# Two product chunks of a feed-forward stage: down products one step later, first factors split early, token halves exchanged, freed banks to the end of the line, two low parts on VectorE

## The chip, the cores and the metric

The kernel runs on one core of one Trainium2 chip. TensorE multiplies, VectorE (DVE in the profile) and ScalarE (ACT) split and combine, GpSimd (POOL) and SyncE (SP) start transfers. The metric is the device time of one execution, in microseconds (us).

## The reference

The program is a trunk of two layers. Each layer is feed-forward, mixer (mLSTM in layer 0, gated MLP in layer 1), feed-forward, gated embedding, each followed by a layer norm. So there are four feed-forward stages, and the change lies in these alone:

```python
def swiglu_ffn(x, w_gu, w_d):
    g, u = jnp.split(x @ w_gu, 2, axis=-1)
    return (jax.nn.silu(g) * u) @ w_d

x = layer_norm(DN_ALPHA * x + 0.5 * swiglu_ffn(x, ffn1_wgu[i], ffn1_wd[i]), ln_g[i, 0], ln_b[i, 0])
```

x has 512 tokens and 1024 columns, the hidden width is 2816. All is float32.

## The kernel before, in words

**Splitting.** A float32 matrix is used as a high and a low part. ScalarE copies the source rounded (whi of a weight, fhi of a factor; L237, L323), VectorE subtracts that from the source (wlo, flo; L246, L324). A product takes three matmuls, high by high, low by high and high by low (`mm3`, L318 to L320). A low can be made without VectorE: ScalarE copies the negated high (L243), and a transfer started by GpSimd adds the source to it (L244). `UP_BY_DMA` lists the weight forms made in that way.

**Weights.** `Weights.order` is one list of all weight tiles in the order in which TensorE takes them. Whenever a tile is released, `fill` splits the next ones in this order until a kind has no free buffer. There are four buffers of the kind main (up weights) and two of the kind rows (down weights). Loads go through three raw buffers (wraw) and five quarters (wquarter), and a raw buffer is loaded anew when the last form made from it is split.

**A feed-forward stage.** The 22 hidden blocks of 128 go through in chunks of 2, 4, 4, 4, 4, 4. While a chunk is projected up, the seven products of the chunk before it go down; these are a Strassen scheme (`Group`: `form` makes and splits a factor, `product` multiplies, `add` puts the result on the residual xt, L687). Down products are called D0 to D6 here. Chunks 0 to 3 are projected plainly. Chunks 4 and 5, here the product chunks, project a pair of blocks in seven products, r0 to r6, and a chunk has two pairs (`UpPair`, `up_products`). So a product chunk has 14 steps s = 0 to 13 of one up product each, and seven of them have a down product too: before, those with even s. The activations' side of the up products is made once at the end of chunk 3 (`UpForms`; its `last` is a row of VectorE work with the tiles x_d, t_wlo and t_f).

**Banks.** r0, r2, r4 and r6 of a pair add into one bank, r3 and r5 into another, r1 has one. After r0, r2 and r3 ScalarE copies the bank out (tile us, L972), after r1, r5 and r4 VectorE adds it to such a copy (L975, L980), ScalarE applies Silu (L976), and VectorE makes h for a half of the tokens by `gated` (L989): after r5 for one half, after r6 for the other. The next product in a bank waits for the copy out of it: r2 for that after r0, r4 for that after r2, r5 for that after r3. In chunk 5 the two halves are split into high and low at once (wquarter, L323, L324). Then `down` multiplies its four blocks plainly, 128 tokens at a time, into dps, after which norm and the next stage follow. The first 128 tokens' dps use the two down banks that `add` of D5 gave free, the second those that `add` of D6 gives free.

**What sets the order.** Nothing is scheduled: each engine runs its instructions in the order in which the Python code emits them, one after the other, and waits at the head of its queue. In `up_products` a step emits the up product, the pending `add`, the copy out or Silu (`take`), the fills of the released up weight, and with a down product that product, the fills of the released down weight, and the next `form`. Both first forms of the next group were emitted at a chunk's end, for chunk 3 behind `UpForms.last`.

Weight forms are made in place on VectorE: s2 (L139, L140) for r2, s3 (L147) for r4, s4 (L151) for r5; for the down weights t2 (L110, L111) for D2 and t1 (L115, L116) for D3.

Of the kernel before, what the change touches and what calls it, by code (L numbers as in the profile page):

```python
# [42 lines left out]
W_BUFS = 4  # L43
EXTRA = 2
PLE_EXTRA = 3
UP_BY_DMA = (1, 2, 4, 5, 6)


class Weights:
# [238 lines left out]
def hybrid_trunk(ctx: ExitStack, tc, x, p, ln_g, ln_b, ffn1_wgu, ffn1_wd, ffn2_wgu, ffn2_wd,  # L288
# [39 lines left out]
    up_held = set()  # L328

    def up_bank(name, hold=False):  # L330
# [7 lines left out]
            return i, bank  # L338
        return bank

    dn_order, pinned = deque(range(4)), {}

    def dn_bank(name, pin=False):
# [57 lines left out]
    def ffn_weights(wgu, wd, name, ple=False):  # L401
# [19 lines left out]
        for c, n in enumerate(FFN_CHUNKS):  # L421
            down_w = deque(forms(c - 1) if c else ())
            if c >= UP_FROM:
                products = []
                for b in range(starts[c], starts[c] + n, 2):
                    products += W.up_forms(*(W.add_load(kp(wgu)[:, :, c0:c0 + 2 * P], 2) for c0 in (b * P, HID + b * P)))
                for s, product in enumerate(products):
                    W.order.append(product)
                    if s % 2 == 0:
                        W.order.append(down_w.popleft())  # L430
                continue
            for i in range(2 * n):
                W.order.append(tiles[2 * starts[c] + i])
                if down_w:
                    W.order.append(down_w.popleft())
# [450 lines left out]
    class UpForms:  # L886
# [52 lines left out]
                          self.quarter(1, 1), self.t4]  # L939

        def quarter(self, k, t):
            return [a[:, 4 * k:4 * k + 4, 256 * t:256 * t + 256] for a in (xh, xl)]

        def step(self):
            if self.steps:
# [2 lines left out]
    class UpPair:  # L948
# [19 lines left out]
        def take(self, r):  # L968
            bank, part = self.bank, self.part
            if r in (0, 2, 3):  # L970
                part[r] = tmp_tile("us").rearrange("p (e c) -> p e c", e=2)
                sca.activation(part[r], bank[3 if r == 3 else 0], AF.Copy)  # L972
            elif r in (1, 5):
                g = part[r // 5 * 2]
                vec.tensor_add(g, g, bank[1 if r == 1 else 3])  # L975
                sca.activation(g, g, AF.Silu)  # L976
                if r == 5:
                    self.gated(1, g, part[3])
            elif r == 4:
                vec.tensor_add(part[3], part[3], bank[0])  # L980
            else:
                self.gated(0, part[0], bank[0])
            if r in (1, 5, 6):
                up_held.remove(self.at[{1: 1, 5: 3, 6: 0}[r]])

        def gated(self, t, g, u):
            s = slice(256 * t, 256 * t + 256)
            h = g if self.h is None else self.h[:, :, s]
            vec.scalar_tensor_tensor(h, g, 0.5, u, op0=OP.mult, op1=OP.mult)  # L989
            if self.h is None:  # L990
# [3 lines left out]
    def ffn(layer, k, rows, late, prepare=None):  # L994
        with stage_pool("forms", 2) as fpool, stage_pool("quarters", Q_BUFS) as qpool, \
# [16 lines left out]

            def up_products(c, n, h):
                nonlocal norm
                pairs = []
                for s in range(7 * n // 2):
                    b, r = s // 7 * 2, s % 7
                    if r == 0:
# [5 lines left out]
                        hs.extend([a[:, e] for a in pair.parts] for e in range(2))  # L1024
                    pair.take(r)
                    W.release()
                    if s % 2 == 0:
                        group.product()
                        W.release(kind="rows")
                        group.form()  # L1030
                    if c == LAST and b == n - 2:
                        if r == 2:
                            W.open("rowsx", late, 1)
                        elif r == 4:
                            norm = Norm(layer, k)

            for c, n in enumerate(FFN_CHUNKS):
                if c < LAST:
# [3 lines left out]
                if c == UP_FROM - 1:  # L1042
                    formed = UpForms(tpool, late)
                if c >= UP_FROM:
                    up_products(c, n, h if c < LAST else None)
                for i in range(2 * n if c < UP_FROM else 0):
                    b = i // 2
                    ps = project()
# [20 lines left out]
                    if formed is not None and i >= FORM_AT:  # L1069
                        formed.step()  # L1070
                        formed.step()
                if c == UP_FROM - 1:
                    while formed.steps:
                        formed.step()
                    formed.last()
                if c < LAST:
                    group = Group(h, fpool, c == 0)
                    group.form()
                    group.form()
# [730 lines left out]
```

## Time and profile before

| | |
|---|---|
| median of 3 runs | 2334.89 us (2334.58 to 2336.22) |
| the profiled execution | 2333.96 us |
| its span, first to last instruction | 2332.2 us |
| TensorE busy, VectorE, ScalarE | 96%, 72%, 46% |
| mean granted TensorE clock | 0.980 |
| product chunks of the four stages begin at | 212.89, 998.79, 1433.56, 2091.42 us |

The trace gives for every instruction its start, its duration and the idle time of its engine before it with what ended that (in brackets). A row with x2 or more merges instructions of one kind that follow each other. TensorE's rows overlap, since its matmuls are pipelined: the distance from start to start is what one costs.

### The profile page before, as it was taken

To read this page: it belongs to the slowest core of one execution; us is meant where nothing else is said; L and a number is where in the kernel's file an instruction comes from. 1 tells how busy PE (TensorE), PEld (TensorE's weight loads), DVE (VectorE), ACT (ScalarE), POOL (GpSimd) and SP (SyncE) were. 2 spreads that over 40 slices of the span, in tenths; PEclk is the share of its full clock that TensorE was granted. 3 is DMA by queue.
4 is the path that set the end of the run, shared out by engine and by line. 5 is a ranking of instruction groups with operands and counts; after the bars stand their busy time and mean duration, and the time that the engine had idled before them with its cause. 6 is when DMAs were issued, how large, how long until landed. Compare 5 with 4: busy or idle time off the path is not lost. (4 is left out here: it accounts for less than half of the span.)

```text
span 2332.2 us, 29478 instructions
## 1 busy us (share of the span) xinstructions
PE 2231.4 (96%) x11669; PEld 1909.1 (82%) x11669; DVE 1678.9 (72%) x2436; ACT 1081.3 (46%) x1508; POOL 172.5 (7%) x215
## 2 busy tenths in 40 slices
PE   9998998999999999989899998898999999999888
PEld 8887887888888888878788887887888888878777
DVE  5668676786776776777786768676788767687777
ACT  4334555564646533355454334554345453346542
POOL 1000110111101000001000000110001000001000
PEclk9999999999999999999999999999999999999999
DMA  6324753556847443356532323753437733346551
GB/s 202 109 82 117 179 112 127 135 128 137 163 113 147 133 130 100 104 122 157 151 122 93 122 70 108 181 131 123 136 90 149 176 101 109 100 118 139 142 161 56
DMA packets 217842, 295.70 MB, mean 127 GB/s; under 512 B 7092, under 2 KB 161844, under 8 KB 217704
## 3 DMA queue, kind: packets, MB, share of 16 engines
q1 hardware_dynamic: 168080, 211.83, 27.9%
q0 software_dynamic: 43008, 67.30, 17.8%
q10 hardware_dynamic: 6616, 14.69, 2.1%
q8 instruction: 92, 1.51, 0.3%
q14 instruction: 46, 0.38, 0.1%
HBM read 224.58 MB, written 2.11 MB: 97 GB/s over the span
## 5 line engine op out<-in xcount | busy, mean ns | idle before, releaser
L237 ACT ACTIVATE whi<-wraw 128x1024 fp32r<-128x1024 f32 (+1 forms) x388 | 400.1, 1047 | 193.4 <-DVE wraw L140 50.4
L246 DVE TENSOR_TENSOR wlo<-wraw,whi 128x1024 fp32r<-128x1024 f32 (+1 forms) x260 | 312.2, 1216 | 81.3 <-ACT whi L237 80.5
L246 DVE TENSOR_TENSOR wlo<-wquarter,whi 128x1024 fp32r<-128x1024 f32 (+1 forms) x140 | 156.4, 1117 | 246.7 <-ACT whi L237 246.5
L318 PE MATMUL fps<-xh,whi 128*128 128x512 f32 x800 | 311.4, 389 | 0.0
L319 PE MATMUL fps<-xl,whi 128*128 128x512 f32 x800 | 311.2, 389 | 0.0
L320 PE MATMUL fps<-xh,wlo 128*128 128x512 f32 x800 | 311.2, 389 | 0.0
L318 PE MATMUL gps<-whi,fhi 128*128 128x512 f32 x644 | 260.0, 404 | 34.9 <-ACT fhi L323 34.9
L320 PE MATMUL gps<-whi,flo 128*128 128x512 f32 x644 | 258.8, 402 | 11.6 <-DVE flo L324 11.6
L319 PE MATMUL gps<-wlo,fhi 128*128 128x512 f32 x644 | 258.3, 401 | 0.0
L244 POOL DMA_DIRECT2D wlo<-wraw x128 | 127.8, 998 | 1560.5 <-ACT wlo L243 1406.2
L237 ACT ACTIVATE whi<-wquarter 128x1024 fp32r<-128x1024 f32 (+1 forms) x140 | 135.7, 969 | 225.2 <-PE gps L320 109.3
L687 DVE TENSOR_TENSOR xt<-xt,gps 128x512 f32<-128x512 f32 x302 | 192.9, 679 | 0.8 <-PE gps L320 0.8
L318 PEld LDWEIGHTS fps<-xh,whi 128*128 128x128 f32 x800 | 150.2, 188 | 31.2
L319 PEld LDWEIGHTS fps<-xl,whi 128*128 128x128 f32 x800 | 150.2, 188 | 31.1
L320 PEld LDWEIGHTS fps<-xh,wlo 128*128 128x128 f32 x800 | 150.1, 188 | 31.1
L318 PEld LDWEIGHTS gps<-whi,fhi 128*128 128x128 f32 x644 | 125.1, 194 | 61.0 <-ACT fhi L323 36.6
L323 ACT ACTIVATE fhi<-h 128x512 fp32r<-128x512 f32 (+1 forms) x140 | 81.1, 582 | 202.3 <-DVE h L852 53.0
L320 PEld LDWEIGHTS gps<-whi,flo 128*128 128x128 f32 x644 | 124.7, 194 | 44.3 <-DVE flo L324 17.3
L318 PE MATMUL ups<-xh,whi 128*128 128x256 f32 x512 | 146.6, 286 | 6.4 <-DVE us L989 4.3
L320 PE MATMUL ups<-xh,wlo 128*128 128x256 f32 x512 | 146.5, 286 | 2.3 <-DMA wlo<-wraw 2.1
L319 PEld LDWEIGHTS gps<-wlo,fhi 128*128 128x128 f32 x644 | 125.3, 195 | 24.9
L319 PE MATMUL ups<-xl,whi 128*128 128x256 f32 x512 | 145.5, 284 | 0.0
(357 smaller groups left out, 4945.4 us busy)
## 6 DMA issues: line engine op xcount, KB each, us to landing
wraw<-in_ffn_wgu_dram SPq DMA_DIRECT2D x79, 1024.0 KB, 7.3
wlo<-wraw POOLq DMA_DIRECT2D x128, 512.0 KB, 5.5
wquarter<-in_ffn_wd_dram SPq DMA_DIRECT2D x64, 512.0 KB, 3.8
wraw<-in_ml_w_in_dram SPq DMA_DIRECT2D x24, 1024.0 KB, 5.9
wraw<-in_gm_w_in_dram SPq DMA_DIRECT2D x15, 1024.0 KB, 5.6
wraw<-in_ffn_wgu_dram SPq DMA_DIRECT2D x17, 512.0 KB, 4.8
wraw<-in_ffn_wd_dram SPq DMA_DIRECT2D x8, 1024.0 KB, 9.1
wraw<-in_ml_w_out_dram SPq DMA_DIRECT2D x8, 1024.0 KB, 5.0
```

Source lines behind the costliest of these rows:

```text
L237: self.nc.scalar.activation(hi[:, s], src[:, s], AF.Copy)
L244: self.nc.gpsimd.dma_start(lo[:, s], src[:, s], accum_op=OP.add)
L246: self.nc.vector.tensor_sub(lo[:, s], src[:, s], hi[:, s].bitcast(F32))
L318: mm(ps, st[0], mv[0], start=start, stop=False, skip_group_check=more)
L319: mm(ps, st[0], mv[1], start=False, stop=False, skip_group_check=more)
L320: mm(ps, st[1], mv[0], start=False, stop=stop, skip_group_check=more)
L323: sca.activation(hi, src, AF.Copy)
L687: vec.tensor_add(dst, dst, ps)
```

## The change

- `UP_BY_DMA` loses forms 5 and 6: the lows of r5 and r6 are subtracted on VectorE. There are two product chunks with two pairs in each of four stages, so 32 lows move.
- In the product chunks the down products (and their weights in `Weights.order`) stand at odd s, one step later. D6 is now the last product of the chunk, and its `add` comes behind the chunk.
- The first factor of the next group is formed early: in chunks 1 to 3 at i = 6, in chunk 4 at s = 12. The second is formed at the chunk's end, for chunk 3 ahead of `UpForms.last`.
- `quarter` and `gated` exchange the token halves: what r5 completes is now tokens 0 to 255.
- `up_let_go` puts a freed up bank at the end of the line, where before its place was that of its last taking.

```diff
-UP_BY_DMA = (1, 2, 4, 5, 6)
+UP_BY_DMA = (1, 2, 4)
...
+    def up_let_go(i):
+        up_held.remove(i)
+        up_order.remove(i)
+        up_order.append(i)
...
                 for s, product in enumerate(products):
                     W.order.append(product)
-                    if s % 2 == 0:
+                    if s % 2:
                         W.order.append(down_w.popleft())
...
         def quarter(self, k, t):
-            return [a[:, 4 * k:4 * k + 4, 256 * t:256 * t + 256] for a in (xh, xl)]
+            return [a[:, 4 * k:4 * k + 4, 256 - 256 * t:512 - 256 * t] for a in (xh, xl)]
...
             if r in (1, 5, 6):
-                up_held.remove(self.at[{1: 1, 5: 3, 6: 0}[r]])
+                up_let_go(self.at[{1: 1, 5: 3, 6: 0}[r]])
...
         def gated(self, t, g, u):
-            s = slice(256 * t, 256 * t + 256)
+            s = slice(256 - 256 * t, 512 - 256 * t)
...
                     pair.take(r)
                     W.release()
-                    if s % 2 == 0:
+                    if s % 2:
                         group.product()
                         W.release(kind="rows")
                         group.form()
+                    if s == 12 and h is not None:
+                        next_group = Group(h, fpool)
+                        next_group.form()
...
                 if c >= UP_FROM:
-                    up_products(c, n, h if c < LAST else None)
+                    next_group = up_products(c, n, h if c < LAST else None)
+                    if c < LAST:
+                        next_group.form()
+                    group.add()
+                    group = next_group
...
+                    if c and i == 6:
+                        next_group = Group(h, fpool)
+                        next_group.form()
+                if c < UP_FROM and c:
+                    group = next_group
+                    group.form()
                 if c == UP_FROM - 1:
                     while formed.steps:
                         formed.step()
                     formed.last()
-                if c < LAST:
+                if c == 0:
                     group = Group(h, fpool, c == 0)
                     group.form()
                     group.form()
```

How this moves the instructions is shown at three places. Line numbers of the changed kernel are larger by 5 from `up_let_go` to `up_products` (L687 is L692, L989 is L994), and by other amounts behind that.

The first is VectorE at the start of chunk 4 of the first stage, behind `UpForms.last`. Before:

```order
L932 TENSOR_TENSOR t_wlo<-x_f_1300,t_whi 128x1024
L324 TENSOR_TENSOR t_f_1754<-x_d,t_f_1753 128x512 x2
L324 TENSOR_TENSOR flo<-h,fhi 128x512 x2
L147 TENSOR_TENSOR wraw<-wraw 128x1024
L110 TENSOR_TENSOR wquarter<-wquarter 128x1024
L111 TENSOR_TENSOR wquarter<-wquarter 128x1024
L246 TENSOR_TENSOR wlo<-wquarter,whi 128x1024
L851 TENSOR_TENSOR h<-h 128x2x256
L852 TENSOR_TENSOR h<-h 128x2x256
L324 TENSOR_TENSOR flo<-h,fhi 128x512
```

The same place in the changed kernel:

```order
L937 TENSOR_TENSOR t_wlo<-x_f_1300,t_whi 128x1024
L324 TENSOR_TENSOR t_f_1762<-x_d,t_f_1761 128x512 x2
L147 TENSOR_TENSOR wraw<-wraw 128x1024
L980 TENSOR_TENSOR us<-us,ups 128x512
L151 TENSOR_TENSOR wraw<-wraw 128x1024
L246 TENSOR_TENSOR wlo<-wraw,whi 128x1024
L110 TENSOR_TENSOR wquarter<-wquarter 128x1024
L111 TENSOR_TENSOR wquarter<-wquarter 128x1024
L246 TENSOR_TENSOR wlo<-wquarter,whi 128x1024
L856 TENSOR_TENSOR h<-h 128x2x256
L857 TENSOR_TENSOR h<-h 128x2x256
L324 TENSOR_TENSOR flo<-h,fhi 128x512
```

Both first flo of the group have gone ahead of this place; the addition after r1 (L980), the form of r5's weight (L151) and its low, which VectorE did not make before, now stand ahead of D2's weight and factor.

The second is ScalarE at the same place, from the first copy out of a bank (us, after r0) to the second (after r2). Before:

```order
L972 ACTIVATE us<-ups 128x512
L237 ACTIVATE whi<-wraw 128x1024
L243 ACTIVATE wlo<-wraw 128x1024
L237 ACTIVATE whi<-wquarter 128x1024
L323 ACTIVATE fhi<-h 128x512
L976 ACTIVATE us<-us 128x512
L237 ACTIVATE whi<-wraw 128x1024
L243 ACTIVATE wlo<-wraw 128x1024
L972 ACTIVATE us<-ups 128x512
```

In the changed kernel:

```order
L977 ACTIVATE us<-ups 128x512
L237 ACTIVATE whi<-wraw 128x1024
L243 ACTIVATE wlo<-wraw 128x1024
L981 ACTIVATE us<-us 128x512
L237 ACTIVATE whi<-wraw 128x1024
L237 ACTIVATE whi<-wquarter 128x1024
L323 ACTIVATE fhi<-h 128x512
L977 ACTIVATE us<-ups 128x512
```

Silu (L981) and the high of r5's weight have moved ahead of D2's weight and factor, one low is gone, and the copy after r2 now follows directly on the factor fhi.

The third is VectorE at the end of chunk 5, up to the first dps on the residual. Before:

```order
L989 SCALAR_TENSOR_TENSOR us<-us 128x512
L324 TENSOR_TENSOR wquarter<-us,wquarter 128x2x256
L246 TENSOR_TENSOR wlo<-wraw,whi 128x1024 x4
L687 TENSOR_TENSOR xt<-xt,gps 128x512 x2
L989 SCALAR_TENSOR_TENSOR us<-us,ups 128x512
L324 TENSOR_TENSOR wquarter<-us,wquarter 128x2x256
L246 TENSOR_TENSOR wlo<-wraw,whi 128x1024
L687 TENSOR_TENSOR xt<-xt,dps 128x512
```

In the changed kernel:

```order
L994 SCALAR_TENSOR_TENSOR us<-us 128x512
L324 TENSOR_TENSOR wquarter<-us,wquarter 128x2x256
L994 SCALAR_TENSOR_TENSOR us<-us,ups 128x512
L324 TENSOR_TENSOR wquarter<-us,wquarter 128x2x256
L246 TENSOR_TENSOR wlo<-wraw,whi 128x1024 x5
L692 TENSOR_TENSOR xt<-xt,gps 128x512 x2
L692 TENSOR_TENSOR xt<-xt,dps 128x512
```

The second half of h is made and split ahead of the weight lows, and the residual of D6 (xt from gps) now comes behind five of them.

More of the change, by code (lines that the diff above doesn't have):

```diff
@@ L1014, in up_products @@
                 nonlocal norm
-                pairs = []
                 for s in range(7 * n // 2):
@@ L1035, in up_products @@
                             norm = Norm(layer, k)
+                return next_group if h is not None else None
             for c, n in enumerate(FFN_CHUNKS):
```

## The prediction

> **What bounds the kernel now.** I read the page's busy times first, then what TensorE waits for, then the queues of TensorE, VectorE and ScalarE through the product chunks.
>
> ```profile
> span 2332.2 us, 29478 instructions
> PE 2231.4 (96%) x11669; PEld 1909.1 (82%) x11669; DVE 1678.9 (72%) x2436; ACT 1081.3 (46%) x1508; POOL 172.5 (7%) x215
> ...
> PE gps L318 <- ACT fhi L323: 34.9, 8, 5.5
> PE dps L318 <- ACT wquarter L323: 21.5, 4, 5.8
> PE gps L320 <- DVE flo L324: 11.6, 8, 2.4
> PE ups L318 <- ACT us L972: 9.1, 14, 1.3
> PE ups L320 <- DMA wlo<-wraw: 8.6, 8, 2.1
> PE ups L318 <- DVE us L989: 4.3, 4, 1.3
> ```
>
> TensorE waits 90.0 us in these six rows (total, times, longest), all inside the product chunks and just behind them. The change aims at each row: a step more before D0 at the factors (34.9 + 11.6), the exchanged halves at the down pass (21.5), VectorE's lows at the transfers (8.6), the bank line at the last row (4.3). Long waits cost more than they show:
>
> ```profile
> 221.45 0.80 PE L318 MATMUL gps<-whi,fhi 128*128 128x512 f32 x1 [5.53 <-ACT fhi L323]
> ...
> 224.43 0.63 PE L319 MATMUL gps<-wlo,fhi 128*128 128x512 f32 x1
> 224.85 0.63 PE L320 MATMUL gps<-whi,flo 128*128 128x512 f32 x1
> ...
> 331.31 0.40 PE L319 MATMUL gps<-wlo,fhi 128*128 128x512 f32 x1
> 331.55 0.39 PE L320 MATMUL gps<-whi,flo 128*128 128x512 f32 x1
> ...
> 335.24 0.39 PE L318 MATMUL ups<-t_whi,whi 128*128 128x256 f32 x1 [1.25 <-ACT us L972]
> 335.46 0.28 PE L319 MATMUL ups<-t_wlo,whi 128*128 128x256 f32 x1
> 335.58 0.28 PE L320 MATMUL ups<-t_whi,wlo 128*128 128x256 f32 x1
> ```
>
> After 5.53 us of waiting a 512-column matmul takes 0.42 from start to start, against 0.24 in a steady stretch; after 1.25 the 256-column ones soon go at 0.12. From these distances 12 matmuls of a down product take 5.0 slow and 2.8 at full speed, so a long wait costs TensorE some 2 to 3 more: with 12 long waits, some 30. If nothing took their place, 120 would go. The Trainium skill ("TensorE: Matmul & The Clock Gate", Part 1) says the same of the half rate, with a window of about 3.4 us for it to come and to go; the rows agree on the rate.
>
> The question is who supplies the product chunks. VectorE, ScalarE and one window:
>
> ```profile
> 222.66 1.29 DVE L324 TENSOR_TENSOR flo<-h,fhi 128x512 fp32r<-128x512 f32 x2
> 223.87 1.22 DVE L147 TENSOR_TENSOR wraw<-wraw 128x1024 f32<-128x1024 f32 x1
> 225.00 1.22 DVE L110 TENSOR_TENSOR wquarter<-wquarter 128x1024 f32<-128x1024 f32 x1
> 226.25 1.22 DVE L111 TENSOR_TENSOR wquarter<-wquarter 128x1024 f32<-128x1024 f32 x1
> 229.22 1.23 DVE L246 TENSOR_TENSOR wlo<-wquarter,whi 128x1024 fp32r<-128x1024 f32 x1 [1.74 <-ACT whi L237]
> 230.36 0.68 DVE L851 TENSOR_TENSOR h<-h 128x512 f32<-128x512 f32 x1
> 231.08 0.69 DVE L852 TENSOR_TENSOR h<-h 128x512 f32<-128x512 f32 x1
> 232.53 0.69 DVE L324 TENSOR_TENSOR flo<-h,fhi 128x512 fp32r<-128x512 f32 x1 [0.76 <-ACT fhi L323]
> ...
> 252.17 0.69 DVE L989 SCALAR_TENSOR_TENSOR h<-us 128x512 f32<-128x512 f32 x1 [0.70 <-ACT us L976]
> 258.36 1.22 DVE L246 TENSOR_TENSOR wlo<-wraw,whi 128x1024 fp32r<-128x1024 f32 x1 [2.50 <-ACT whi L237]
> ...
> 294.07 1.22 DVE L147 TENSOR_TENSOR wraw<-wraw 128x1024 f32<-128x1024 f32 x1
> ```
>
> ```profile
> 225.12 1.06 ACT L237 ACTIVATE whi<-wraw 128x1024 fp32r<-128x1024 f32 x1 [2.72 <-DVE wraw L147]
> 226.08 1.04 ACT L243 ACTIVATE wlo<-wraw 128x1024 fp32r<-128x1024 f32 x1
> ...
> 231.86 0.63 ACT L323 ACTIVATE fhi<-h 128x512 fp32r<-128x512 f32 x1 [2.68 <-DVE h L852]
> ...
> 238.16 0.58 ACT L972 ACTIVATE us<-ups 128x512 f32<-128x512 f32 x1
> ```
>
> ```profile
> 223.87:294.07 70.20, 63.60 (x421) 57.71 (x421) 48.71 (x59) 39.45 (x48) 8.41 (x10) 0.94 0.65 158
> ```
>
> From r4's weight form (L147) of chunk 4 to that of chunk 5 is one turn, 70.20 us, VectorE busy 48.71 of it. Its idle time is a ping-pong: it forms, ScalarE rounds, it subtracts, each at the head of its queue.
>
> **The change part by part.** A low in VectorE's queue costs 1.14 from start to start (229.22 to 230.36).
>
> *Lows back on VectorE.* 32 x 1.14 = 36.5 of VectorE's time, 4.6 a turn. ScalarE loses 32 copies of 0.96 (225.12 to 226.08) and GpSimd 32 transfers; SyncE's loads keep their order, and those into the raw buffers of these lows start no later, since VectorE subtracts at once where a transfer had to land. r5's low is worse than its 1.14: it follows its own form (L151), so VectorE stands still while ScalarE rounds (1.06, as at 225.12).
>
> *Products later, factors early.* D0's factor is ready before TensorE asks for it: that row goes. But r0, D0, r1, r2, D1, r3 still stand ahead of r4, in another order, and r4 waits for the copy out of r2's bank, which follows D2's weight and factor on ScalarE. I walk the changed order with the rows' durations. Two flo (1.2) leave VectorE's stretch before L147 and the low of D1's weight (1.14) comes in, so L147 starts at about 223.2 (222 to 225, between all and none of this being hidden). Then L147 1.14, the addition 0.6, L151 1.22; until ScalarE has rounded r4's weight, copied its negative, applied Silu and rounded r5's weight it is 228.0; the low 1.14, L110 and L111 2.5: 231.6; rounding 1.2, low 1.14, two ops on h 1.4: 235.4; fhi 0.7, copy 0.6: 236.6. Before, the copy ended at 238.74. TensorE, having had D0 at once, reaches r4 at 230.5 and waits 6 us: the wait at D0 has become one at r4 ("ups from ACT us"), half-speed stretch included. Behind it TensorE's whole queue waits, and nobody else but through it.
>
> *The turn.* VectorE works 48.7 + 4.6 = 53.3. Its waits on the walk: r5's two roundings 1.9 + 1.2, D2's and D3's 1.2 each, three h factors at 0.76, two Silu at 0.70, two stretches of rounding, negated copy and rounding at 3.1 (0.6 longer than the 2.50 at 258.36), one of 2.7 before the early factor, 1.9 at D0's next weight, which waits for D5, and 0.4 of small ones: 20.4. Sum 73.7 against 70.20: **+3.5 a turn**. TensorE needs less: at 2.87 an up product (24 x 0.12) and 2.75 a down product, 14 x 2.87 + 7 x 2.75 = 59.4. So VectorE with ScalarE is the bound.
>
> *The end of chunk 5.* L147 of chunk 5 comes at 223.2 + 73.7 = 296.9. r4 of the second pair goes 50.2 behind it on the walk (13.4 to the first copy as above, 24.6 more through the weights and factors of D3 and D4 to the second pair's L147, 12.2 more through D5's weight and the form and rounding of r5), plus 3.0 for two high-low pairs of h (about 1.5 each): 350.1. Then r4, D5, r5, r6, D6 follow without a wait: 3 x 2.87 + 2 x 2.75 = 14.1, D6 ends at 364.2. The first dps finds its halves ready: the 21.5 go.
>
> ```profile
> 212.89 0.28 PE L318 MATMUL ups<-xh,whi 128*128 128x256 f32 x1
> ...
> 367.26 0.80 PE L318 MATMUL dps<-whi,wquarter 128*128 128x512 f32 x1 [5.84 <-ACT wquarter L323]
> ...
> 372.07 0.39 PE L318 MATMUL dps<-whi,wquarter 128*128 128x512 f32 x1
> ...
> 998.79 0.28 PE L318 MATMUL ups<-xh,whi 128*128 128x256 f32 x1
> ...
> 1154.24 0.39 PE L318 MATMUL dps<-whi,wquarter 128*128 128x512 f32 x1
> ...
> 2091.42 0.28 PE L318 MATMUL ups<-xh,whi 128*128 128x256 f32 x1
> ...
> 2248.10 0.63 PE L318 MATMUL dps<-whi,wquarter 128*128 128x512 f32 x1
> ```
>
> The rows at 372.07, 1154.24 and 2248.10 are the second 128 tokens of the first, second and fourth stage, the ups rows the stages' first up products. The second 128 tokens need the bank that D6's residual frees, which now stands behind five lows: rounding 1.2, five lows 5.7, the addition 0.7: 364.2 + 7.6 = 371.8, while TensorE is there 24 matmuls of 0.23 behind D6, at 369.7. So 371.8 against 372.07; with the turn 0 to 1.8 longer where a half-speed stretch reaches into D5, +0.5. The third stage has the same weights order as the first and is taken like it: **+0.5 each**. In the second and fourth stage rows buffers also take the turned p, so the first down weight itself is split only after D6, and six lows precede the residual: 151.3 + 0.8 (half speed) + 8.7 = 160.8 after the stage's first up product, against 1154.24 - 998.79 = 155.45 and 2248.10 - 2091.42 = 156.68: **+5.3 and +4.1**.
>
> *Exchange and bank line.* The exchange moves no work; its gain is the factor and the dps above. The bank line takes away the 4.3, which lie within the slack that TensorE now has; worth 0 here. Chunks 1 to 3: TensorE waits there for nothing in the rows, so the earlier factor gains 0; its cover is the plain up product ahead of it (24 matmuls of 512 columns, 24 x 0.23 = 5.5), and without that it would cost what D0 cost, 5.5.
>
> Sum: 0.5 + 0.5 + 5.3 + 4.1 = 10.4. The profiled execution took 2333.96 (span 2332.2 and 1.8 around it), so 2344.4; the median is 0.93 above that execution: **2345**.
>
> **Rivals.**
> *Hidden lows (faster).* The lows may fit into VectorE's idle 21.5 of a turn: ScalarE makes four copies fewer a turn, 3.8. Then the turn stays 70.2, and two turns a stage give back 2 x 3.5 x 4 = 28: 2317. For it: that idle time; against it: VectorE's waits are for ScalarE's answer to its own last form, which fewer copies do not hasten. Half hidden would be 2331. Its far end is nothing in place of all waits: 2345 - 10 - 120 = 2215. The Trainium skill ("Perfetto Trace Analysis", Identifying the Most-Contended Engine) takes the engine with the highest occupancy for the bound and would close its gaps, which are this change's; by that TensorE, busy 82 to 96%, decides and this rival holds.
> *No bank wait (same).* If the residual of D6 does not hold the second 128 tokens, 2.1 go in two stages and about 0.7 in the others: 2345 - 5.6 = 2339.
> *Half speed on the chain (slower still).* D0's weight of chunk 5 waits for D5. If the slow stretch after r4's wait lasts through D5 in both chunks, 0.9 a turn comes on top, 4 x 2 x 0.9 = 7: 2352.
>
> **How the numbers follow.** Slower as walked, 2341 to 2349: 0.42. Half speed: 0.18. Same: 0.22. Hidden lows: 0.18, of which 0.04 for the far end. A measurement of this kernel can tell about 0.2%, 4.7, from no change. So faster 0.18, same 0.22, slower 0.60. The likeliest is 2345. The range runs from 2324, where three quarters of the lows are hidden, to 2359, the half-speed case with L147 at its late bound, 1.8 in each of four stages; it leaves out the deeper hidden cases, about 0.1, and less above.
>
> **What would show it.** Right: "ups from ACT us" grows from 9.1 to some 80 with single waits of 4 to 6, at r4 of the first pair and r2 or r4 of the second; the gps rows from fhi and flo, and dps from wquarter vanish; "dps waits for xt" appears with about 2 us, two or four times; L147 to L147 takes 73 to 75; VectorE is busy 1715, ScalarE 1050. Wrong: a turn under 71, or "ups from ACT us" below 30: then the lows were hidden. If the turn is right but the second dps comes early, it is the bank.

## The result and the profile after

The changed kernel takes 2349.78 us (median of 4, 2348.57 to 2351.28), the kernel before 2335.51 beside it (4 runs, 2334.58 to 2336.22): a ratio of 1.0062, 95% interval 1.0044 to 1.0079. The change makes the kernel slower by 14.3 us, where 10 were forecast.

The page after, with its span, its busy times and then all TensorE waits of ups, gps and dps of 1 us or more (us in total, times, longest):

```profile
span 2347.4 us, 29405 instructions
PE 2234.5 (95%) x11669; PEld 1922.8 (82%) x11669; DVE 1716.2 (73%) x2468; ACT 1051.8 (45%) x1476; POOL 145.0 (6%) x183
...
PE ups L318 <- ACT us L977: 89.9, 24, 5.9
PE dps L318 <- DVE xt L692: 6.0, 4, 2.4
PE dps L318 <- ACT whi L237: 2.4, 2, 1.2
PE ups L318 <- DVE us L985: 2.1, 3, 0.8
PE dps L319 <- DVE wlo L246: 1.5, 2, 0.8
```

Of the six rows of before, the five that the change aimed at, 80.9 us (90.0 less 9.1), are gone. The sixth has taken their place: TensorE waits 89.9 for the copy us (L972 before, L977 now), where it waited 9.1. Another 9.9 have come at the second 128 tokens and at the first down weight of `down`. In all TensorE waits 11.9 longer than before (101.9 against 90.0).

TensorE's queue in the first stage: its first up product, the waits at r4 of both pairs of chunk 4 and at the first r4 of chunk 5, then the first dps and the second 128 tokens. The three `ups` rows with a wait are those three products r4:

```profile
212.98 0.28 PE L318 MATMUL ups<-xh,whi 128*128 128x256 f32 x1
...
236.70 0.58 PE L318 MATMUL ups<-xh,whi 128*128 128x256 f32 x1 [5.93 <-ACT us L977]
...
273.50 0.58 PE L318 MATMUL ups<-xh,whi 128*128 128x256 f32 x1 [5.69 <-ACT us L977]
...
311.51 0.58 PE L318 MATMUL ups<-xh,whi 128*128 128x256 f32 x1 [3.94 <-ACT us L977]
...
365.67 0.39 PE L318 MATMUL dps<-whi,wquarter 128*128 128x512 f32 x1
...
373.43 0.50 PE L318 MATMUL dps<-whi,wquarter 128*128 128x512 f32 x1 [2.16 <-DVE xt L692]
```

r4 waits 5.93 us in the first pair, 5.69 in the second, 3.94 in chunk 5. The first dps (365.67) and those behind it now find their halves split: the 21.5 are gone. (In the kernel before, that wait stood behind twelve matmuls of dps, which began at 358.51 in this stage.) The second 128 tokens wait 2.16 for the residual of D6.

VectorE and ScalarE at three places of the walk:

```profile
223.30 1.22 DVE L147 TENSOR_TENSOR wraw<-wraw 128x1024 f32<-128x1024 f32 x1
...
367.01 5.77 DVE L246 TENSOR_TENSOR wlo<-wraw,whi 128x1024 fp32r<-128x1024 f32 x5 [0.70 <-ACT whi L237]
372.70 1.27 DVE L692 TENSOR_TENSOR xt<-xt,gps 128x512 f32<-128x512 f32 x2
```

```profile
236.07 0.58 ACT L977 ACTIVATE us<-ups 128x512 f32<-128x512 f32 x1
```

L147 stands at 223.30, the copy for r4 ends at 236.65 (236.07 + 0.58), and the residual (xt from gps, 372.70) stands behind five lows.

The four turns, from L147 of chunk 4 to L147 of chunk 5, those of the first and third stage: window, length, busy times of PE, PEld, DVE, ACT and POOL, then clock, DMA share and GB/s. The last row has the sum and the mean:

```profile
223.30:298.05 74.75, 63.13 (x409) 58.96 (x407) 53.42 (x63) 35.88 (x44) 5.03 (x6) 0.91 0.47 120
...
1451.96:1525.21 73.25, 61.65 (x408) 57.72 (x408) 53.42 (x63) 35.88 (x44) 5.12 (x6) 0.93 0.48 122
...
sum 296.30, PE 249.11 PEld 232.49 DVE 213.69 ACT 143.51 POOL 20.32; mean PE 62.28 PEld 58.12 DVE 53.42 ACT 35.88 POOL 5.08
```

A turn is 74.75 in the first stage, 73.25 in the third, on average 74.1 (296.30 by four), VectorE busy 53.4 of it. The same sum for the kernel before is the basis of all that follows:

```profile
sum 278.86, PE 253.21 PEld 230.43 DVE 194.81 ACT 158.10 POOL 33.93; mean PE 63.30 PEld 57.61 DVE 48.70 ACT 39.53 POOL 8.48
```

That is 69.7 a turn, busy 48.7. VectorE's idle time is the difference: 21.0 before (278.86 - 194.81, by four), 20.7 after. It has 4.7 more work and hardly less waiting.

### The profile page after: what moved, and what is told of

Its sections match the earlier page's. It is cut to its first block, busy times and chain, and to the rows that moved or that the text cites. A ratio compares the mean times of both kernels' runs of the same rounds, so it can differ in the third digit from the quotient of the medians.

```text
span 2347.4 us, 29405 instructions
## 1 busy us (share of the span) xinstructions
PE 2234.5 (95%) x11669; PEld 1922.8 (82%) x11669; DVE 1716.2 (73%) x2468; ACT 1051.8 (45%) x1476; POOL 145.0 (6%) x183
## 4 chain that ended last, share of the span: by engine, by line
PE 76%; DVE 12%; ACT 6%; issue 4%; DMA 0%; ACTq 0%; POOL 0%; DVEq 0%; POOLq 0%
PE fps L318 8%; PE fps L320 7%; PE fps L319 7%; PE gps L318 5%; PE gps L319 5%; PE gps L320 5%; DVE wlo L246 3%; ACT whi L237 3%; PE ups L318 2%; PE dps L318 2%; PE dps L320 2%; PE dps L319 2%; PE ups L319 2%; PE ups L320 2%; DVE xt L692 2%
## 5 line engine op out<-in xcount | busy, mean ns | idle before, releaser
L246 DVE TENSOR_TENSOR wlo<-wraw,whi 128x1024 fp32r<-128x1024 f32 (+1 forms) x292 | 350.0, 1217 | 81.3 <-ACT whi L237 80.5
L318 PE MATMUL gps<-whi,fhi 128*128 128x512 f32 x644 | 253.0, 393 | 0.0
L319 PE MATMUL gps<-wlo,fhi 128*128 128x512 f32 x644 | 252.1, 392 | 0.0
L320 PE MATMUL gps<-whi,flo 128*128 128x512 f32 x644 | 251.3, 390 | 0.0
L318 PE MATMUL ups<-xh,whi 128*128 128x256 f32 x512 | 158.9, 310 | 70.4 <-ACT us L977 70.4
L244 POOL DMA_DIRECT2D wlo<-wraw x96 | 100.6, 1048 | 1576.1 <-ACT wlo L243 1493.4
L692 DVE TENSOR_TENSOR xt<-xt,gps 128x512 f32<-128x512 f32 x302 | 193.0, 679 | 0.7 <-PE gps L320 0.7
L318 PEld LDWEIGHTS ups<-xh,whi 128*128 128x128 f32 x512 | 110.1, 215 | 76.3 <-ACT us L977 75.4
L319 PE MATMUL ups<-xl,whi 128*128 128x256 f32 x512 | 156.1, 305 | 0.0
L320 PE MATMUL ups<-xh,wlo 128*128 128x256 f32 x512 | 155.9, 304 | 0.0
```

The source lines that it names most:

```text
L244: self.nc.gpsimd.dma_start(lo[:, s], src[:, s], accum_op=OP.add)
L246: self.nc.vector.tensor_sub(lo[:, s], src[:, s], hi[:, s].bitcast(F32))
L318: mm(ps, st[0], mv[0], start=start, stop=False, skip_group_check=more)
L319: mm(ps, st[0], mv[1], start=False, stop=False, skip_group_check=more)
L320: mm(ps, st[1], mv[0], start=False, stop=stop, skip_group_check=more)
L692: vec.tensor_add(dst, dst, ps)
```

## The experiments

Two theories stood after the result. The first is that of the prediction: the lows on VectorE cost the turn. The rival: the order costs it. Ratios are against the kernel before, run beside each on the same chip (its medians 2336.1 to 2337.0), with 95% intervals. Beside the changed kernel its median was 2335.5, so a difference between two of these runs is sure to some 2 us.

**The lows back to the transfers**, all else as changed:

```diff
-UP_BY_DMA = (1, 2, 4)
+UP_BY_DMA = (1, 2, 4, 5, 6)
```

> The changed kernel with the lows of r5 and r6 back on transfers, all else as changed. Theory (VectorE's and ScalarE's queues bound the product chunks and the two lows lengthen them): VectorE does 4.6 us less in a turn and no longer stands still behind r5's form, but ScalarE copies four times more, 3.8; walked for the first half turn, r4 of the first pair starts 2.9 earlier than in the changed kernel, r6 2.0 earlier. With 2 us a turn, eight turns: 2350 - 16 = 2334 us, 2328 to 2340. Rival (the later down products alone cost it, the lows lie in idle time): no change against the changed kernel, 2346 to 2352.

Measured: 2347.7 us, ratio 1.0043 (1.0029 to 1.0056). The intervals of this run and of the changed kernel overlap; the lows are worth some 2 us of the 14 (4 by the ratios), and the first theory's 2334 is not reached. r4 waits 3.0 only, as the walk without the two lows has it, but r4 of the second pair waits 6.6: a negated copy (L243, at 270.85) now stands on ScalarE ahead of the copy that it waits for. The last row sums the four turns of this run:

```profile
233.79 0.39 PE L318 MATMUL ups<-xh,whi 128*128 128x256 f32 x1 [2.99 <-ACT us L977]
...
272.43 0.58 PE L318 MATMUL ups<-xh,whi 128*128 128x256 f32 x1 [6.64 <-ACT us L977]
...
sum 291.36, PE 247.75 PEld 230.70 DVE 195.31 ACT 158.29 POOL 33.98; mean PE 61.94 PEld 57.68 DVE 48.83 ACT 39.57 POOL 8.49
```

A turn is 72.8 (291.36 by four), VectorE busy 48.8 and idle 24.0. So of the 4.4 by which the changed kernel's turn is longer than before (74.1 for 69.7), 3.1 are there without the lows, and the lows add 1.2: the other 3.4 of their 4.6 are taken out of idle time.

**The lows alone**, in the kernel before:

```diff
-UP_BY_DMA = (1, 2, 4, 5, 6)
+UP_BY_DMA = (1, 2, 4)
```

> The kernel before with one edit, the lows of r5 and r6 on VectorE. Theory: VectorE takes 4.6 us more a turn, part of which ScalarE's four copies fewer give back; 1 us a turn and more: 2342 us, 2338 to 2348, slower than before. Rival (the lows lie in VectorE's idle time; the waits for their transfers, 8.6 us, go): faster than before, 2325 to 2331.

Measured: 2319.87, ratio 0.9924 (0.9911 to 0.9936). Faster by 17 us, beyond what even the rival gave: the first theory falls.

```profile
PE dps L318 <- ACT wquarter L323: 13.1, 4, 3.8
...
sum 276.10, PE 252.14 PEld 230.67 DVE 213.41 ACT 143.82 POOL 20.36; mean PE 63.03 PEld 57.67 DVE 53.35 ACT 35.95 POOL 5.09
```

VectorE works 4.7 more a turn, as was counted, but stands idle 15.7 instead of 21.0 (276.10 - 213.41, by four), so the turn is 69.0, 0.7 shorter than before. Most of the gain comes later: from each stage's first up product to its first dps the four stages together take 4.0 us less, and from there to the last dps 10.4 less, since the wait for the split halves has fallen from 21.5 to 13.1 and with it the half speed behind. Where the idle time went shows in VectorE's queue. The kernel before waits twice long for the high of a down weight, and once for the load of an up weight:

```profile
241.60 1.22 DVE L246 TENSOR_TENSOR wlo<-wquarter,whi 128x1024 fp32r<-128x1024 f32 x1 [3.06 <-ACT whi L237]
...
270.88 1.23 DVE L246 TENSOR_TENSOR wlo<-wquarter,whi 128x1024 fp32r<-128x1024 f32 x1 [4.04 <-ACT whi L237]
...
283.21 1.23 DVE L139 TENSOR_TENSOR wraw<-wraw 128x1024 f32<-128x1024 f32 x1 [1.88 <-DMA wraw<-in_ffn_wgu_dram]
```

With the lows alone the two places of the down weights read:

```profile
243.69 1.23 DVE L246 TENSOR_TENSOR wlo<-wquarter,whi 128x1024 fp32r<-128x1024 f32 x1 [1.19 <-ACT whi L237]
...
270.80 1.23 DVE L246 TENSOR_TENSOR wlo<-wraw,whi 128x1024 fp32r<-128x1024 f32 x1 [1.88 <-ACT whi L237]
271.94 1.22 DVE L246 TENSOR_TENSOR wlo<-wquarter,whi 128x1024 fp32r<-128x1024 f32 x1
```

Of the waits of 3.06 and 4.04, 1.19 (at 243.69) and none (at 271.94) are left in front of these down weights. Lows of up weights (from wraw) have taken their places: two ahead of the first, with 1.19 and 0.21 of waiting, so that little is gained there, and one ahead of the second, with 1.88. Before, ScalarE made a negated copy of the up weight ahead of the down weight's high; now that copy is gone, and VectorE has the low to do while ScalarE rounds. The wait for the load is gone too; over the four turns it was 1.7 a turn, so nearly a third of the 5.3 is no answer of ScalarE's at all. How the gain divides between fewer copies and work in the place of a wait is read from these rows, not tried apart.

**The exchange alone**, in the kernel before:

```diff
-            return [a[:, 4 * k:4 * k + 4, 256 * t:256 * t + 256] for a in (xh, xl)]
+            return [a[:, 4 * k:4 * k + 4, 256 - 256 * t:512 - 256 * t] for a in (xh, xl)]
...
-            s = slice(256 * t, 256 * t + 256)
+            s = slice(256 - 256 * t, 512 - 256 * t)
```

> The kernel before with one edit, the token halves exchanged. Theory: the first dps finds its halves, so the waits of 4.7 to 5.8 us and the half-speed stretch behind them go in all four stages; the second 128 tokens then wait some 1 us for the bank that D6's residual frees (its residual ends at 365.4 in the first stage, TensorE would be there at 364.0, and was there at 372.07): 6 to 7 us a stage, 2335.5 - 26 = 2310 us, 2305 to 2316. Rival (the half that now comes last, or the bank, holds the down pass as long as before): 2330 to 2336.

Measured: 2319.75, ratio 0.9925 (0.9913 to 0.9938), between the two, 17 us faster. The row of dps waiting for wquarter is gone from the waits.

So two parts of the change gain 17 us each by themselves, and the whole loses 14. One of the other parts must cost some 48, or the gains must not add up.

**The residual first.** In the changed kernel D6's residual was put ahead of the fills that D6's release starts:

```diff
                         group.product()
+                        if h is None and s == 13:
+                            group.add()
                         W.release(kind="rows")
```

> The changed kernel with the residual of D6 in chunk 5 emitted ahead of the weight lows that follow D6, instead of behind them. Theory: the waits of dps for xt, 2.2, 0.8, 2.4 and 0.8 us, go and nothing else moves: 2350 - 6 = 2344 us, 2342 to 2347. Rival (another wait, of the third and fourth block's weights, takes their place, since their lows come 1.2 later): 2348 to 2352.

Measured: 2342.14, ratio 1.0022 (1.0013 to 1.0030): 7.6 us less than the changed kernel. The prediction's bank wait is real; its rival without that wait priced it at 5.6, 2 too little.

**The later products alone**, in the kernel before:

```diff
-                    if s % 2 == 0:
+                    if s % 2:
                         W.order.append(down_w.popleft())
...
-                    if s % 2 == 0:
+                    if s % 2:
                         group.product()
...
                     up_products(c, n, h if c < LAST else None)
+                    group.add()
```

> The kernel before with one part of the change alone: down products and their weights at odd s (the last add behind the chunk); lows, exchange, early factor and bank line as before. Theory, revised after the first four: the later products are what costs, since Silu, form and low of r5 and D2's weight and factor come ahead of the copies out of the banks; the two lows and the exchange, each worth 16 to 17 us by itself, are gains that the change keeps. If these add up, 14.3 + 17 + 16 = 47 us lie in the later products with the early factor: 2365 to 2385 us here, waits of TensorE for the copy us above 80. Rival, the early factor costs it: 2328 to 2345 here, since the later products give D0 a step more. Second rival, nothing adds up and the later products only hide what the lows and the exchange bring: 2335 to 2352.

Measured: 2345.22, ratio 1.0035 (1.0022 to 1.0047): 8.5 us slower, not 30 to 50. The parts do not add up; the second rival held. Its waits:

```profile
PE ups L318 <- DVE us L989: 16.6, 4, 5.3
PE ups L318 <- DVE h L989: 15.7, 5, 3.9
PE ups L318 <- DVE us L980: 15.6, 8, 3.0
PE ups L318 <- ACT us L972: 13.4, 7, 2.9
PE gps L318 <- ACT fhi L323: 11.1, 5, 2.6
...
sum 287.63, PE 258.44 PEld 237.31 DVE 195.23 ACT 157.33 POOL 33.92; mean PE 64.61 PEld 59.33 DVE 48.81 ACT 39.33 POOL 8.48
```

The wait for the factor fhi has shrunk from 34.9 to 11.1, and dps no longer waits for wquarter, without any exchange. But ups waits 61.3 for the additions, h and the copies, and VectorE's idle time is 23.1 a turn.

**Even steps**, all else as changed:

```diff
-                    if s % 2:
+                    if s % 2 == 0:
                         W.order.append(down_w.popleft())
...
-                    if s % 2:
+                    if s % 2 == 0:
                         group.product()
```

> The changed kernel with the down products and their weights back at even s; lows on VectorE, exchange, early first factor and bank line stay. Theory (later products cost): the gains of lows and exchange are seen, 2336 - 17 - 16 = 2303, and less where the early factor takes away TensorE's wait at D0: 2288 to 2308 us. Rival (early factor costs): 2328 to 2348. Second rival (gains do not add up, each takes the same wait): 2312 to 2322.

Measured: 2308.91, ratio 0.9878 (0.9862 to 0.9893): 41 us below the changed kernel by this edit alone, 1 us above the range of the revised theory.

**The early factor alone**, in the kernel before, products at even s. The expectation counts the bank line in, but the edit leaves it out: `up_let_go` is defined there and never called, so freed banks keep the places that they had before. Its main lines:

```diff
+                    if s == 12 and h is not None:
+                        next_group = Group(h, fpool)
+                        next_group.form()
...
+                    if c and i == 6:
+                        next_group = Group(h, fpool)
+                        next_group.form()
```

> The kernel before with the early factors alone (and the bank line): first factor of the next group at i = 6 or s = 12, the second at the chunk's end ahead of the last row of forms; products at even s, lows and halves as before. Theory (later products cost): the wait at D0 of chunk 4 goes or shrinks (34.9 us of waits for the factor in all, with half speed behind it), 2318 to 2330 us. Rival (early factor costs): 2350 to 2380. No effect, because the factor that comes early only moves the wait on to the copy out of the bank: 2332 to 2340.

Measured: 2340.66, ratio 1.0016 (1.0007 to 1.0025), 4 us slower, nearest to no effect: D0 of chunk 4 no longer waits, but r4 does, 6.89 for the copy. The early factor is not the cost.

**Even steps with the residual first**: the run with even steps, and the last add ahead of the fills at s = 12.

```diff
                         group.product()
+                        if h is None and s == 12:
+                            group.add()
                         W.release(kind="rows")
```

> As the run with even steps, and in the last chunk the residual of D6 is put ahead of the fills that D6 frees, so that the second 128 tokens' banks come free sooner. Both theories: 0 to 8 us under the run with even steps, as far as its second dps waits for xt; as the last of the four it is the candidate that beats both kernels: 2282 to 2305 us by the theory, 2322 to 2346 by the rival of the early factor.

Measured: 2306.00, ratio 0.9871 (0.9858 to 0.9885), 1 us above the range that the theory gave. This version beats both kernels, by 30 and 44 us. The largest row of its waits, and its turns:

```profile
PE ups L318 <- ACT us L977: 62.6, 21, 5.9
...
sum 275.42, PE 240.27 PEld 222.06 DVE 213.29 ACT 143.11 POOL 20.34; mean PE 60.07 PEld 55.51 DVE 53.32 ACT 35.78 POOL 5.09
```

68.9 a turn, VectorE busy 53.3, idle 15.5. TensorE's longest wait for a copy is as long as in the changed kernel (5.9), but all of them come to 62.6 instead of 89.9.

**Fills behind the copy.** In the changed kernel, at odd s as it is, the fills and the next factor that follow a down product were put behind the copy out of the bank (or the addition) of the next even step:

```diff
+                    if s and s % 2 == 0:
+                        W.release(kind="rows")
+                        group.form()
                     if s % 2:
                         group.product()
-                        W.release(kind="rows")
-                        group.form()
...
+                W.release(kind="rows")
                 return next_group if h is not None else None
```

> The changed kernel, products at odd s as they are, with the fills that a down product frees and the next factor put one step later, behind the copy out of the bank (or the addition) of the next even step. Theory (place in the queue: TensorE waits at r4 because the copy after r2 stands behind D2's weight and factor in ScalarE's queue): the four waits of a stage for the copy us (5.9, 5.7, 3.9, 4.4) go or fall under 2, and half to all of the 41 us that lie between the changed kernel and the run with even steps come back: 2308 to 2330 us. Rival (it is the whole ping-pong of VectorE and ScalarE that sets the turn, wherever the copies stand): the waits move to the down products' factors, the turn stays at 73 to 75, 2343 to 2355.

Measured: 2337.99, ratio 1.0008 (0.9999 to 1.0017): 12 of the 41 us. Both theories missed it. The wait at r4 is gone, but r5 has one:

```profile
238.76 0.58 PE L318 MATMUL ups<-xh,whi 128*128 128x256 f32 x1 [4.25 <-ACT us L977]
```

```profile
237.60 0.63 ACT L323 ACTIVATE fhi<-h 128x512 fp32r<-128x512 f32 x1 [2.87 <-DVE h L857]
238.13 0.58 ACT L977 ACTIVATE us<-ups 128x512 f32<-128x512 f32 x1
```

r5 waits for the copy after r3 (238.13), which now stands behind the factor fhi. The turn is 72.4 (289.48 by four) and VectorE idle 18.7: a third of the way from 74.1 and 20.7 to the 68.9 and 15.5 at even s. The copy's place in ScalarE's queue is a part of the cost, not the whole.

**Two without the early factor**: the version with even steps and the residual first (2306.00), and the changed kernel, both with the two factors of the next group formed at the chunk's end as before. The edit is this and its counterpart in chunks 1 to 3:

```diff
-                    if s == 12 and h is not None:
-                        next_group = Group(h, fpool)
-                        next_group.form()
```

> The run with even steps and the residual first (2306.0 us), without the early factor: both factors of the next group are formed at the chunk's end as before. If the early factor alone costs or gives nothing (it cost 4 us by itself in the old order): 2298 to 2308. If the early factor is what lets lows and exchange add up: 2316 to 2324, as either of these by itself.

Measured, at even s: 2308.21, ratio 0.9881 (0.9867 to 0.9894), at the upper end of the first range.

> The changed kernel without the early factor: products at odd s, lows, exchange, bank line. Theory (the later products by themselves take back what lows and exchange bring): 2336 to 2352 us, the early factor within 8 of nothing. Rival (later products cost only together with the early factor, which stands ahead of the last row of forms and in the place of a wait): 2312 to 2328, since the later products by themselves cost 8.5 and lows and exchange gain 17 each.

Measured, at odd s: 2353.54, ratio 1.0076 (1.0062 to 1.0090), 1.5 us above the theory's range. The early factor gives 2 to 4 us here, and in both orders the intervals with and without it overlap. So the rival that it costs together with the later products falls, and the later products are what costs.

**The changed kernel without the exchange**: both slices as before.

> The changed kernel with the token halves as before. Theory (exchange and later products remove one and the same wait, that of the first dps for its split halves; once the products are later, the second removal brings nothing): 2344 to 2354 us, against 2349.8 of the changed kernel. Rival (the exchange is worth its 17 us in either order): 2362 to 2370, with the wait of dps for wquarter back at 15 to 22 us in all.

Measured: 2350.66, ratio 1.0066 (1.0052 to 1.0079), within the interval of the changed kernel. None of its waits is for wquarter, and its waits for the copy us come to 89.6, like the changed kernel's. The later products remove the same wait as the exchange, so there the exchange has nothing left to remove.

Laid together (medians, us; in brackets with the residual first):

| | products at even s | products at odd s |
|---|---|---|
| nothing else | 2336 | 2345.2 |
| with lows, exchange, bank line | (2308.2) | 2353.5 |
| and the early factor | 2308.9 (2306.0) | 2349.8 (2342.1) |

The later step costs 9 us by itself and 41 in this company. In the old order lows, exchange, bank line and residual first bring 28 together; in the new one lows, exchange and bank line cost 8.

## Why the prediction was right, and where it was not

**The walk** held. L147 was put at 223.2 and came at 223.30; the copy's end at 236.6, and came at 236.65; r4's wait at 6, and was 5.93. "Ups from ACT us" was to be some 80 and is 89.9. VectorE is busy 1716.2 for 1715, ScalarE 1051.8 for 1050.

**The turn** held as a sum, 73.7 against 74.1 (work 53.3 and 53.4, waits 20.4 and 20.7). Its attribution failed. The step says "VectorE works 48.7 + 4.6", with the idle time as a ping-pong that cannot take up the lows, and against the rival of hidden lows "fewer copies do not hasten" ScalarE's answers. In the old order the lows alone take 5.3 of the 21.0 idle away, add 4.7 of work, and the kernel gains 17. In the new order they take 3.4 of 24.0 away and add 1.2 to the turn (72.8 without them, 74.1 with). So the step that failed is the split of the turn's +3.5: the lows were charged with it, and *Products later, factors early* was counted as a wait that moves from D0 to r4, at no price in the turn. It is the later products that make the turn longer: by 2.2 when they come alone (71.9 for 69.7), and by 5.2 with all else as changed (74.1 for the 68.9 of the run with even steps). What differs shows in VectorE's groups over the first turn: the lows of the up weights (from wraw), those of the down weights (from wquarter), and those of the factors; behind each the busy time, the mean, and the idle time before them. The changed kernel:

```profile
L246 DVE TENSOR_TENSOR wlo<-wraw,whi 128x1024 fp32r<-128x1024 f32 x8 | 9.7, 1220 | 3.2 <-ACT whi L237 3.2
...
L246 DVE TENSOR_TENSOR wlo<-wquarter,whi 128x1024 fp32r<-128x1024 f32 x7 | 8.6, 1223 | 11.6 <-ACT whi L237 11.6
L324 DVE TENSOR_TENSOR flo<-h,fhi 128x512 fp32r<-128x512 f32 x7 | 4.8, 688 | 4.9 <-ACT fhi L323 4.9
```

The run with even steps and the residual first:

```profile
L246 DVE TENSOR_TENSOR wlo<-wraw,whi 128x1024 fp32r<-128x1024 f32 x8 | 9.7, 1222 | 5.8 <-ACT whi L237 5.8
...
L246 DVE TENSOR_TENSOR wlo<-wquarter,whi 128x1024 fp32r<-128x1024 f32 x7 | 8.6, 1223 | 5.5 <-ACT whi L237 5.5
L324 DVE TENSOR_TENSOR flo<-h,fhi 128x512 fp32r<-128x512 f32 x7 | 4.8, 688 | 2.3 <-ACT fhi L323 2.3
```

The work is the same. Ahead of the down weights' lows VectorE waits 11.6 at odd s and 5.5 at even s, ahead of the factors' 4.9 and 2.3; only the up weights' lows wait longer at even s, 5.8 for 3.2. Single rows say how:

```profile
250.71 1.23 DVE L140 TENSOR_TENSOR wraw<-wraw 128x1024 f32<-128x1024 f32 x1
255.04 1.23 DVE L246 TENSOR_TENSOR wlo<-wquarter,whi 128x1024 fp32r<-128x1024 f32 x1 [3.10 <-ACT whi L237]
```

```profile
255.65 1.22 DVE L140 TENSOR_TENSOR wraw<-wraw 128x1024 f32<-128x1024 f32 x1
256.79 0.68 DVE L994 SCALAR_TENSOR_TENSOR h<-us,ups 128x512 f32<-128x512 f32 x1
259.97 1.23 DVE L246 TENSOR_TENSOR wlo<-wraw,whi 128x1024 fp32r<-128x1024 f32 x1 [2.51 <-ACT whi L237]
261.12 1.22 DVE L246 TENSOR_TENSOR wlo<-wquarter,whi 128x1024 fp32r<-128x1024 f32 x1
```

At odd s (first fence) the down weight's low comes right behind r2's form, with 3.10 of standing still in between. At even s (second fence) h is made and an up weight's low stands between, and the down weight's low needs no wait. Over the four turns that is 20.7 of idle time at odd and 15.5 at even s, 5.2 a turn; two turns a stage and four stages would make 42 of it. The runs that differ in this alone are 41 apart (2349.8 and 2308.9), and 36 with the residual first in both (2342.1 and 2306.0). The second turn, taken from L147 of chunk 5 to the first dps, is 69.2 on average of the four stages in the changed kernel and 64.5 in the run with even steps, so it differs by 4.7. With 0.7 less ahead of the first turn, the changed kernel's four stages take 36.4 longer up to the first dps, of the 39.2 by which the spans of these two differ (2347.4 and 2308.2). So the cost lies in the two turns. That the order of the fills does it is read from the rows; the run with the fills behind the copy moved 12 of the 41 and shows that the place of two copies is some of it. What makes up the rest was not taken apart.

**The exchange** was given the 21.5 of the first dps. They are gone, but the run without the exchange shows that the later products take them away alone. Nothing in the forecast's sum hung on which.

**The end of chunk 5** was right in mechanism and too small. The first dps comes at 365.67 for 364.2, the second 128 tokens at 373.43 for 371.8. From each stage's first up product the second 128 tokens come at 160.45 in the first stage (373.43 - 212.98), 161.41 in the second (1161.67 - 1000.26), 160.76 in the third and 162.54 in the fourth. Before it was 159.18, 155.45, 159.15 and 156.68. So +1.3, +6.0, +1.6 and +5.9, in all 14.7, where +0.5, +5.3, +0.5 and +4.1 were forecast: each of the four terms of the sum was too small, by 0.7 to 1.8. Behind them stand two larger amounts: up to the first dps the four stages take 36.7 us longer than before, and from there to the last dps 22.2 less, since the waits for the split halves and the half speed behind them are gone. Removing the wait for the residual alone gave 7.6.

**Half speed**, a rival of 0.18, makes up the missing 1.0 of the first stage's turn (74.75 for 73.7). The wait at r4 of the second pair ends at 273.50 in stage 1 and at 1502.15 in stage 3. TensorE's granted clock around these two ends (window, length, busy times of PE, PEld, DVE, ACT and POOL, then the clock, DMA share and GB/s):

```profile
272.80:276.21 3.41, 2.71 (x12) 2.71 (x13) 3.01 (x3) 3.41 (x6) 0.00 (x0) 0.50 0.20 48
276.21:279.62 3.41, 3.41 (x16) 3.24 (x15) 3.41 (x5) 1.83 (x3) 0.00 (x0) 0.50 1.07 359
279.62:283.03 3.41, 3.41 (x21) 2.95 (x19) 0.69 (x2) 2.09 (x3) 0.83 (x1) 1.00 0.83 247
...
1501.60:1505.01 3.41, 2.86 (x13) 2.86 (x14) 3.16 (x3) 3.41 (x7) 0.00 (x0) 0.50 0.25 62
1505.01:1508.42 3.41, 3.41 (x22) 3.06 (x21) 3.41 (x6) 2.84 (x3) 0.00 (x0) 1.00 1.00 315
```

In stage 1 the clock is at half up to 279.62, which is inside D5, in stage 3 only up to 1505.01, inside r4. From the ends of the waits that is 6.1 and 2.9 us, and the turns are 74.75 and 73.25. Half of 3.2 more at half speed is 1.6, and the turns differ by 1.5. The second and fourth stage fit in between, with 3.9 and 5.8 us and turns of 73.73 and 74.57. The forecast's rival allowed 0.9 a turn for this; two of the four stages had it. Which ones is chance as far as the walk goes: it depends on where the wait falls in the clock's own steps, as the last section shows. Against the walk's 73.7 the four turns are 0.4 longer on average.

The rival of the hidden lows is the one that the runs treat most oddly. Its premise held in the kernel before, and for most of the lows in the changed one; its time, 2317, did not, since it left out what the later products cost. The Trainium skill ("Perfetto Trace Analysis", Identifying the Most-Contended Engine) would look to the engine with the highest occupancy, and for TensorE to the busy share of the weight loads in place of that of the matmuls. By that nothing tells the kernel before from the changed one: the matmuls are busy 96% and 95%, the weight loads 82% in both. VectorE's work and idle time in a turn do, 48.7 and 21.0, 53.4 and 20.7, and 53.3 and 15.5 in the version of 2306 us.

**Not settled**: the bank line was never tried alone. Between lows and bank line, what cost 8 in the new order without the early factor is open.

## What to carry to other kernels

Idle time of an engine that answers another is no fixed price: count for each wait what could stand in front of it, in the order as it will be, before calling work on that engine a cost. Price the parts of a bundle in the old order as well as in the new one, since two parts may remove the same wait, and one may take away the gap that hid another. Where a change moves a step, look first at which forms and fills it brings next to each other in the queues of the engines that answer.

## What the runs showed of the hardware

After the eight waits of 5.7 to 5.9 us of the changed kernel, TensorE runs at half speed for 2.9 to 6.1 us. The granted clock in its trace shows why this varies. Before the program's end it is at 0.5 in 17 stretches, twelve of 6.83 us and five of 3.41, and all of them begin on one grid with steps of 3.41 us, wherever a wait ends: those at 235.25 and 272.80 are eleven steps apart. So a part of the slow time can lie inside the wait (1020.32 to 1027.14, where the wait ends at 1023.98), or it can begin after it: behind the wait of 3.93 that ends at 1097.76 the matmuls first go at full speed, and the clock is at half from 1098.82 to 1102.24.

Which step is slow goes, in these records, with how long TensorE stood idle in the step before it. (Idle is what TensorE's rows show in brackets.) In this trace every step at full clock with 1.91 us idle or more is followed by one at half clock, and none with 1.82 or less is. A step at half clock is followed by a full one where TensorE stands idle for up to 0.55 us in it, and by another at half clock from 0.70 on. In all 14 traces the first bound lies between 1.6 and 1.95 us, the second between 0.4 and 0.6. So a wait of 2.75 us (ending at 1578.61) cost a step at half clock, with 1.91 of it in one step, and one of 2.35 (ending at 1602.40) cost none. This is read from the traces; no run was made to try it.

The Trainium skill ("TensorE: Matmul & The Clock Gate", Part 1) gives about 3.4 us for a window that runs freely, and the trace agrees in both. It names an idle window as the condition for half rate; here somewhat more than half of a window was enough.
